# Queue order in a hybrid DeltaNet/attention block: weight splits paced by the piece in use, gate Silu behind attention, decayed keys before the inverse, normed outputs turned later

## The chip, the cores and the metric

The kernel runs on one core of one Trainium2 chip. The metric is the device time of one execution in microseconds (us); lower is better. The core has TensorE (PE, matmuls, with its weight loads shown apart as PEld), VectorE (DVE), ScalarE (ACT), GpSimd (POOL) and SyncE (SP, which here only issues DMAs). Each engine works through its own queue in order. Which engine does a thing is written in the kernel; in which order the instructions lie in a queue is settled when the program is built, by a scheduler that takes earlier parts of the program first where several are ready.

## The reference, cut to what matters

One residual block over 512 tokens of width 1024, in float32:

```python
x = x + 0.5 * g1 * swiglu(modulate(x, sh1, s1), ffn1_w_in, ffn1_w_out)
h = modulate(x, sh2, s2)                       # RMSNorm * (1 + scale) + shift
proj = h @ w_in                                # splits: gq gk gv gz ga gb cq ckv kr
# group A, gated DeltaNet, 4 heads of 128
q, k, v = silu(causal_conv(gq, gk, gv));  q, k = l2norm(q), l2norm(k)
o_a = gated_delta_rule(q, k, v, g, beta)       # chunk form: inverse, u = T v, w = T k, recurrence over chunks
o_a = rms(o_a, gdn_norm_w) * silu(gz)
# group B, latent attention, 4 heads, block-causal
o_b = rms(softmax(q_b k_b^T) v_b, mla_out_norm_w)
x = x + g2 * (concat(o_a, o_b) @ w_out)
x = x + 0.5 * g3 * swiglu(modulate(x, sh3, s3), ffn2_w_in, ffn2_w_out)
```

The FFN width is 2816. (shift, scale, gate) come from a linear map of silu(c).

## The kernel before, in words

Activations lie transposed: a tile holds 128 features by 512 tokens. The dense products keep float32 accuracy by splitting each operand into a rounded high part (`fp32r`) and the rest: `mm3` (L302) makes three matmuls for each pair of tiles, high by high, high by low and low by high. A weight piece ("unit", 1024 rows by 128 columns) is loaded by SP into `wr`, and `split_w` (L201) makes it two pieces: a cast on ACT (`wh`, L202) and a subtraction on DVE (`wl`, L203). Each of the three tags has four buffers. `next_unit` (L298) splits the next unit ahead in program order just before it returns the current one; where the split really lies in the queues of ACT and DVE is the scheduler's choice. A dense piece is 24 matmuls (L304 to L306).

The stages in order: FFN1; then the mixer; then FFN2. Within the mixer (L1666) the projection units run in the order latents, keys, queries, values, z gate. While they run, `dense_units` (L971) steps three side lists of generators: `chain` (latent lifts, delta keys and decay, the blockwise inverse, the solves), `deltas` (query products and norms) and `att` (attention). Steps are traced between pieces of dense work, so that PE has something of each.

After the four z units a loop (L1756) runs `chain`, `deltas` and `rest` (attention) until the first two solves are traced, adds steps of `fill` (the output projection of the attention heads, `out_attended`, L1803; one step is three matmuls of 512 columns), and traces the Silu of the four z tiles when attention has been traced in full (`gate_silu`, L1749). Table activations (Exp, Silu) are chained in program order by `table` (L175), so that few table loads are needed.

Then comes the recurrence over four blocks of 128 tokens (L1776 to L1799). Its matmuls keep the order in which they are traced (`matmuls_in_order`, L153). For block p, `recur` (L1402) has two halves: first `w S` and `q S` (L1415, L1423), then the state update and the output (L1430, L1438). After each half come fill steps and steps of `gated`, a list of `gated_out` generators (L1446), one for each block: the first step takes squares and an inverse root (ACT, DVE, and `ry` by pow on POOL, L188); the second scales the output (`on`, DVE, L969); the third turns it on PE (four transposes, L1461), multiplies by gain and gate (`mf`, L1467) and splits it into `mh` and `ml` (L1469, L1470). The generator yields once more after that, so its end takes a fourth step. `gated` and every list of this kind steps its open generators in turn; one that is at its end is dropped by the step that finds it so.

`solve` (L1370) makes for block p the weighted values `vb`, then (for p > 0) the decayed keys `kbg` and (for p < 3) `kd`, all three DVE products recorded at the helper's line L969, then the products with the inverse (L1389, L1398), copied by ACT to `uu` (L1391) and `w` (L1400).

The output projection of the DeltaNet heads follows in two halves of 256 tokens: `out_half` (L1829) inside the recurrence's fill and final flush, `out_rest` (L1843) behind it. A tile of `out_half` is 12 matmuls of 256 columns; two tiles share one wide unit.

`follow` (L137) adds an edge of class NoSync from one instruction to another: it constrains the order in which the queues are laid out, and no semaphore is made for it.

## Time and profile before

| | |
|---|---|
| median of 3 runs | 1080.29 us (1079.97 to 1081.68) |
| the profiled execution | 1081.6 us; span from first to last instruction 1079.9 us |
| mean granted TensorE clock | 0.997 |
| idle time of PE in the span | 22 us of 1079.9 |
| mixer's stages, us from the span's start | latents and lifts 403 to 487; queries, values, z gate with attention and inverse to about 620; end of attention and solves to 649; recurrence to 684; output halves to about 710; then FFN2 |

A row of a group reads: line, engine, operation, what is written and read, count, then busy time and mean duration of one, then the idle time of the engine just before and who ended it. A row of the waits reads: who waited, for whom, us in total, how often, the longest. A row of the timeline reads: start, duration, engine, line, operation, tiles, count, and in brackets the engine's idle time before it and what ended that. Matmuls are pipelined, so a matmul's duration is longer than the distance to the next one's start.

### The profile page before, as it was taken

What the parts mean: (1) busy time and instruction counts of PE and PEld (TensorE: products, weight loads), DVE (VectorE), ACT (ScalarE), POOL (GpSimd) and SP (SyncE); (2) the same over time, 40 slices, a digit from 0 to 9 for tenths busy, and PEclk for the clock granted to TensorE, in tenths of its full rate; (3) what the DMA queues carried; (4) which work ended last, traced back from release to release, by engine and by line L of the source; (5) the groups of instructions that cost most, each with busy time, mean ns of one, the idle gap of its engine ahead of it and who ended that gap; (6) DMA issues with size and microseconds to landing.
All of it is one profiled execution on the core that took longest, in us unless ns stands there. A gap on an engine that the chain in (4) does not pass through costs nothing.

```text
span 1079.9 us, 14096 instructions
## 1 busy us (share of the span) xinstructions
PE 1057.4 (98%) x5601; PEld 881.9 (82%) x5601; DVE 566.7 (52%) x1000; ACT 383.9 (36%) x641; POOL 25.8 (2%) x74
## 2 busy tenths in 40 slices
PE   6999999999999999999999989999999999999998
PEld 4788878788887798888788778998888888888887
DVE  4478983433586437559797477573333333322220
ACT  3342222222222226465855553352222222222220
POOL 1000000000000000100000002000000000000000
PEclk8999999999999999999999999999999999999999
DMA  9979973233697335210332121004333333333320
GB/s 273 276 219 317 291 217 107 80 96 93 202 289 260 93 88 162 79 39 20 79 88 55 38 75 41 26 22 135 98 98 97 96 95 95 90 100 108 100 71 30
DMA packets 207760, 130.59 MB, mean 121 GB/s; under 512 B 13633, under 2 KB 191822, under 8 KB 207694
## 3 DMA queue, kind: packets, MB, share of 16 engines
q1 hardware_dynamic: 207694, 129.69, 41.2%
q8 instruction: 44, 0.72, 0.3%
q14 instruction: 22, 0.18, 0.1%
HBM read 127.18 MB, written 2.49 MB: 120 GB/s over the span
## 4 chain that ended last, share of the span: by engine, by line
PE 91%; DVE 5%; ACT 1%; DMA 1%; POOL 1%; issue 1%; SPq 0%; ACTq 0%; POOLq 0%
PE pa L304 26%; PE pa L306 26%; PE pa L305 26%; PE pb L1635 1%; PE pb L1615 1%; DMA ar<-in_w_ada 1%; PE pb L305 1%; PE pb L304 1%; PE pb L306 1%; PE pb L453 1%; PE pb L527 1%; PE pb L1237 1%; POOL ry L188 1%; DVE cv L1181 1%; DVE wl L203 0%
## 5 line engine op out<-in xcount | busy, mean ns | idle before, releaser
L202 ACT CAST wh<-wr 128x1024 fp32r<-128x1024 f32 (+1 forms) x164 | 166.9, 1020 | 482.9 <-PE pa L305 322.7
L304 PE MATMUL pa<-hh,wh 128*128 128x512 f32 (+1 forms) x837 | 324.9, 388 | 0.4 <-DVE cv L1181 0.4
L306 PE MATMUL pa<-hh,wl 128*128 128x512 f32 (+1 forms) x837 | 322.0, 385 | 1.4 <-DVE wl L203 1.4
L305 PE MATMUL pa<-hl,wh 128*128 128x512 f32 (+1 forms) x837 | 321.8, 384 | 1.1 <-DVE hl L490 1.1
L203 DVE TENSOR_TENSOR wl<-wr,wh 128x1024 fp32r<-128x1024 f32 (+1 forms) x164 | 194.3, 1187 | 231.1 <-ACT wh L202 225.4
L304 PEld LDWEIGHTS pa<-hh,wh 128*128 128x128 f32 x837 | 157.4, 188 | 34.3 <-issue 2.9
L306 PEld LDWEIGHTS pa<-hh,wl 128*128 128x128 f32 x837 | 157.4, 188 | 32.5 <-DVE wl L203 2.1
L305 PEld LDWEIGHTS pa<-hl,wh 128*128 128x128 f32 x837 | 157.5, 188 | 30.5 <-DVE hl L490 1.4
L304 PE MATMUL pa<-ah,wh 128*128 128x512 f32 (+1 forms) x396 | 146.3, 370 | 0.0
L306 PE MATMUL pa<-ah,wl 128*128 128x512 f32 (+1 forms) x396 | 144.9, 366 | 0.0
L305 PE MATMUL pa<-al,wh 128*128 128x512 f32 (+1 forms) x396 | 144.8, 366 | 0.0
L304 PEld LDWEIGHTS pa<-ah,wh 128*128 128x128 f32 x396 | 74.7, 189 | 13.5 <-ACT wh L202 1.7
L306 PEld LDWEIGHTS pa<-ah,wl 128*128 128x128 f32 x396 | 74.7, 189 | 12.2
L305 PEld LDWEIGHTS pa<-al,wh 128*128 128x128 f32 x396 | 74.7, 189 | 11.9
L658 DVE TENSOR_TENSOR af<-sg,pa 128x512 f32<-128x512 f32 x40 | 27.5, 686 | 103.0 <-PE pa L306 103.0
L612 DVE SCALAR_TENSOR_TENSOR aa<-ar,sc,aa 128x512 f32<-128x512 f32 x98 | 73.2, 750 | 14.5 <-DMA ar<-in_w_ada 13.4
L720 DVE SCALAR_TENSOR_TENSOR xT<-pa,mod,xT 128x512 f32<-128x512 f32 (+1 forms) x18 | 12.4, 692 | 50.1 <-PE pa L306 49.9
L660 ACT CAST ah<-af 128x512 fp32r<-128x512 f32 x44 | 27.4, 622 | 19.7 <-DVE af L658 19.7
L304 PE MATMUL pa<-mh,wh 128*128 128x256 f32 (+1 forms) x96 | 32.6, 341 | 0.0
L305 PE MATMUL pa<-ml,wh 128*128 128x256 f32 (+1 forms) x96 | 30.9, 322 | 0.3 <-DVE ml L1663 0.3
L661 DVE TENSOR_TENSOR al<-af,ah 128x512 fp32r<-128x512 f32 x44 | 30.2, 686 | 1.5 <-ACT ah L660 1.4
L306 PE MATMUL pa<-mh,wl 128*128 128x256 f32 (+1 forms) x96 | 30.7, 320 | 0.0
(375 smaller groups left out, 1076.9 us busy)
## 6 DMA issues: line engine op xcount, KB each, us to landing
wr<-in_ffn_w_in SPq DMA_DIRECT2D x79, 512.0 KB, 3.9
ar<-in_w_ada SPq DMA_DIRECT2D x48, 512.0 KB, 6.2
wr<-in_ffn_w_out SPq DMA_DIRECT2D x32, 512.0 KB, 4.1
ar<-in_w_ada SPq DMA_DIRECT2D x48, 256.0 KB, 5.1
wr<-in_w_in SPq DMA_DIRECT2D x21, 512.0 KB, 3.8
wr<-in_ffn_w_out SPq DMA_DIRECT2D x16, 384.0 KB, 4.5
wr<-in_w_out SPq DMA_DIRECT2D x8, 512.0 KB
wr<-in_ffn_w_in SPq DMA_DIRECT2D x8, 384.0 KB, 7.3
```

What stands on the lines that cost most here:

```text
L188: nc.gpsimd.tensor_tensor(out=y, in0=v, in1=self.mhalf[:, :n], op=ALU.pow)
L202: self.nc.scalar.copy(hi, raw)
L203: self.nc.vector.tensor_tensor(out=lo, in0=raw, in1=hi.bitcast(F32), op=ALU.subtract)
L304: mm(out, wh, xh, start=start, stop=False)
L305: mm(out, wh, xl, start=False, stop=False)
L306: mm(out, wl, xh, start=False, stop=stop)
L453: nc.tensor.matmul(pg[32 * q:32 * q + 32, :256], self.sc[:, kc:kc + 1].to_broadcast([P, 32]), a[:, kc], start=(e == 0), stop=(e == 1), til ...
L612: nc.vector.scalar_tensor_tensor(out=acc, in0=a, scalar=sc, in1=acc, op0=ALU.mult, op1=ALU.add)
L658: nc.vector.tensor_tensor(out=a, in0=s, in1=pu, op=ALU.mult)
L660: nc.scalar.copy(ah, a)
L661: nc.vector.tensor_tensor(out=al, in0=a, in1=ah.bitcast(F32), op=ALU.subtract)
L720: nc.vector.scalar_tensor_tensor(out=self.xT[t][:, ts], in0=p[:, ts], scalar=gate[:, t:t + 1], in1=self.xT[t][:, ts], op0=ALU.mult, op1=AL ...
```

## The change

Four things, all in the order of queues; no arithmetic is added or dropped.

1. From the latents' first three pieces on (`paced`), the cast and the subtraction of each weight split follow the last dense matmul traced so far (`dense_mm`).
2. The Silu of the z tiles follows the last activation of the attention heads' output (`att_end`).
3. The decayed keys `kbg` and `kd` leave `solve` for a generator of their own, `decayed_keys`, added to `deltas` before the loop of L1756; `solve` waits in tracing until they have been traced.
4. In the recurrence `gated` is stepped once per half of `recur` instead of twice, ahead of the fill steps instead of behind them; after the last block it is stepped once more, and then five fill steps instead of four come ahead of the flush.

```diff
-    def table(self, *args, **kw):
+    def table(self, *args, after=None, **kw):
         ins = self.nc.scalar.activation(*args, **kw).ins
+        if after:
+            self.follow(ins, after)
...
     def split_w(self, raw, hi, lo):
-        self.nc.scalar.copy(hi, raw)
-        self.nc.vector.tensor_tensor(out=lo, in0=raw, in1=hi.bitcast(F32), op=ALU.subtract)
+        a = self.nc.scalar.copy(hi, raw)
+        b = self.nc.vector.tensor_tensor(out=lo, in0=raw, in1=hi.bitcast(F32), op=ALU.subtract)
+        if self.paced:
+            self.follow(a.ins, self.dense_mm)
+            self.follow(b.ins, self.dense_mm)
...
-        mm(out, wl, xh, start=False, stop=stop)
+        self.dense_mm = mm(out, wl, xh, start=False, stop=stop).ins.name
...
             ps = self.first_units([self.next_unit(ahead=0) for _ in range(3)], (0, 0, 2), norms)
+        self.paced = True
...
+    def decayed_keys(self):
+        h4 = lambda x: x.rearrange("p (h d) -> p h d", h=4)
+        for p in range(NB):
+            c4 = slice(4 * p, 4 * p + 4)
+            if p > 0:
+                self.kbg[p] = self.slot(s="kbg")
+                self.mul(h4(self.kbg[p]), h4(self.kt[p]), self.bc(self.eG[:, c4], 4))
+            if p < NB - 1:
+                self.kd[p] = self.slot(s="kd")
+                self.mul(h4(self.kd[p]), h4(self.kt[p]), self.bc(self.kcd[:, c4], 4))
+            self.turned = p + 1
+            yield
...
-        kt = self.kt[p]
-        if p > 0:
-            kbg = self.slot(s="kbg")
-            self.mul(h4(kbg), h4(kt), self.bc(self.eG[:, c4], 4))
-        if p < NB - 1:
-            self.kd[p] = self.slot(s="kd")
-            self.mul(h4(self.kd[p]), h4(kt), self.bc(self.kcd[:, c4], 4))
+        while self.turned <= p:
+            yield
+        kbg = self.kbg[p]
         yield
...
-        nc.scalar.activation(mh, pt, AF.Copy, scale=gain)
+        self.att_end = nc.scalar.activation(mh, pt, AF.Copy, scale=gain).ins.name
...
+        deltas.add(self.decayed_keys())
         gates = list(self.zT)
 
         def gate_silu(n):
-            silu(gates[:n])
+            silu(gates[:n], self.att_end)
...
                 for _ in self.recur(p):
                     loosely(chain, 2)
                     loosely(rest, 4)
+                    gated.step()
                     if not rest.open and not rest.todo:
                         fill.step(3)
-                    gated.step(2)
                 gated.add(self.gated_out(p))
                 gated.step()
...
             while rest.open or rest.todo:
                 loosely(rest, 1)
-            fill.step(4)
+            gated.step()
+            fill.step(5)
             gated.flush()
             fill.flush()
```

More of the change, by code (lines that the diff above doesn't have):

```diff
@@ L102, in __init__ @@
         self.tabled = None
+        self.paced = False
     def name(self, s):
@@ L1684, in conv_done, with silu @@
             return f
-        def silu(tiles):
+        def silu(tiles, after=None):
             for t in tiles:
-                self.table(t, t, AF.Silu)
+                self.table(t, t, AF.Silu, after=after)
         self.inv = [None] * NB
-        self.kd, self.us, self.o, self.wk = ([None] * NB for _ in range(4))
+        self.kd, self.kbg, self.us, self.o, self.wk = ([None] * NB for _ in range(5))
+        self.turned = 0
         self.S = None
```

## The prediction, made before the change was run

> **What bounds the kernel now.** I read the page first: busy shares and groups.

> ```profile
> span 1079.9 us, 14096 instructions
> PE 1057.4 (98%) x5601; PEld 881.9 (82%) x5601; DVE 566.7 (52%) x1000; ACT 383.9 (36%) x641; POOL 25.8 (2%) x74
> L202 ACT CAST wh<-wr 128x1024 fp32r<-128x1024 f32 (+1 forms) x164 | 166.9, 1020 | 482.9 <-PE pa L305 322.7
> L203 DVE TENSOR_TENSOR wl<-wr,wh 128x1024 fp32r<-128x1024 f32 (+1 forms) x164 | 194.3, 1187 | 231.1 <-ACT wh L202 225.4
> ```

> TensorE (PE) is busy 98% of the span, and the change takes no matmul away. All that can be won is the 22 us in which PE is idle, and all that can be lost is new idle time. So the second view is the waits of PE alone, of which these rows belong to the mixer:

> ```profile
> PE pb L1461 <- DVE on L969: 1.9, 3, 1.0
> PE pb L1635 <- ACT pT L1631: 1.7, 1, 1.7
> PE pa L306 <- DVE wl L203: 1.4, 1, 1.4
> PE pb L1657 <- DVE on L969: 0.8, 1, 0.8
> PE pb L1389 <- DVE vb L969: 0.8, 2, 0.4
> PE pa L304 <- DVE cv L1181: 0.4, 1, 0.4
> PE pa L305 <- DVE ml L1663: 0.3, 1, 0.3
> ```

> Together 7.3 us: the ceiling of any gain, 0.7% of the time. The third view is the windows by stage (columns: PE, PEld, DVE, ACT, POOL busy, clock, DMA share and rate):

> ```profile
> 441.00:487.00 46.00, 46.00 (x229) 39.60 (x229) 23.16 (x52) 27.25 (x52) 2.00 (x2) 1.00 0.17 46
> 487.00:517.00 30.00, 29.36 (x146) 23.19 (x144) 29.37 (x85) 16.79 (x32) 1.02 (x1) 1.00 0.07 18
> 597.00:649.00 52.00, 48.37 (x409) 37.96 (x409) 30.79 (x65) 28.94 (x61) 2.01 (x2) 1.00 0.22 62
> 740.00:1040.00 300.00, 300.00 (x1335) 248.41 (x1334) 96.91 (x102) 80.50 (x102) 0.00 (x0) 1.00 0.34 99
> ```

> PE idles in 487 to 517 (where DVE is busy 29.37 of 30 us: DVE bounds that stretch) and 3.6 us in 597 to 649. From 740 to 1040, FFN2, it has no idle time at all. The L1461 waits lie in the recurrence after that.

> **Gate Silu behind the attention.** On ACT, and PE's row after it:

> ```profile
> 621.31 1.28 ACT L177 ACT_TABLE_LOAD   x1
> 622.61 2.19 ACT L177 ACTIVATE z<-z 128x512 f32<-128x512 f32 x4
> 625.23 0.35 ACT L1631 COPY pT<-pb 128x256 f32<-128x256 f32 x1
> 625.63 0.71 PE L1635 MATMUL pb<-vn,pT 128*128 128x128 f32 x4 [1.67 <-ACT pT L1631]
> 635.83 0.69 ACT L1662 ACTIVATE mh<-pb,cwT 128x512 fp32r<-128x512 f32 x1 [4.36 <-PE pb L1657]
> 640.21 0.58 ACT L1391 COPY uu<-pb 128x512 f32<-128x512 f32 x1 [0.54 <-PE pb L1389]
> ```

> The table load and four Silus hold ACT for 3.5 us (621.31 to 624.80) with attention's copies queued behind them; PE waits 1.7 for one. Tied behind the last L1662 they start some 1.7 earlier than 636.5 and are over by 638.3, about when the first uu copy, then also 1.7 earlier (638.5), wants ACT. Queued behind them are only splits that nobody waits for yet, and z is first read by the turned outputs of the recurrence. Cover gone, it would cost up to the block, 3.5; I take none. Gain 1.7. Two later waits of attention, 0.8 and 0.3, have a chain that begins at those copies; PE arrives earlier too, so I take 0.3 of 1.1.

> **Decayed keys ahead of the inverse.** Three kd and three kbg products:

> ```profile
> L969 DVE TENSOR_TENSOR kbg<-ktk,eG x3: 674/676/676, 640.5 to 645.9; 128x512 f32<-128x512 f32 x3
> L969 DVE TENSOR_TENSOR kd<-ktk,kcd x3: 673/677/677, 639.3 to 643.5; 128x512 f32<-128x512 f32 x3
> ```

> They are 4.1 us of DVE between the vb products that PE awaits. `deltas` steps once a turn, so they go to the first turns, and DVE has 21 idle us in 597 to 649 to take them. They hold two slots more than before (each replaces its ktk, but blocks 1 and 2 need both). The vb waits go: gain 0.8. If the slots delay attention it could be nothing.

> **Normed outputs turned later.**

> ```profile
> 661.65 1.22 DVE L203 TENSOR_TENSOR wl<-wr,wh 128x1024 fp32r<-128x1024 f32 x1
> 661.82 1.92 POOL L188 TENSOR_TENSOR ry<-ve,mhalf 128x4 f32<-128x4 f32 x1 [1.11 <-DVE ve L1452]
> 673.88 0.66 PE L1461 MATMUL pb<-ident,on 128*128 128x128 f32 x4 [0.97 <-DVE on L969]
> 678.71 1.01 POOL L188 TENSOR_TENSOR ry<-ve,mhalf 128x4 f32<-128x4 f32 x1 [5.61 <-DVE ve L1452]
> 680.59 0.63 PE L1461 MATMUL pb<-ident,on 128*128 128x128 f32 x4 [0.30 <-DVE on L969]
> 678.69 0.28 PE L304 MATMUL pa<-mh,wh 128*128 128x256 f32 x1
> 678.81 0.28 PE L305 MATMUL pa<-ml,wh 128*128 128x256 f32 x1
> ```

> Following the generators: `gated_out` has three yields and its end takes a fourth step. With single steps, block 0 is scaled in `recur(1)`'s first half and turned after its second; block 0's end eats a step, so block 1 is turned in `recur(3)`'s first half, blocks 2 and 3 only in the final flush. Each L1461 group then has at least a half of `recur` and three fill steps more between it and its product: over 2 us against waits of 0.97 at most. Block 3 gets one tile of out_half more: 12 matmuls at 0.12 (678.69 to 678.81), 1.4, against 0.30. Gain 1.9.

> Here one pow takes 1.92 beside a weight subtraction and 1.01 alone. [...]

> The price lies behind it: out_half's splits. Unit 97's split may now only follow tile 1 and is needed at tile 4, while blocks 2 and 3 bring DVE this:

> ```profile
> L1467 DVE SCALAR_TENSOR_TENSOR mf<-pb,cwT,z x16: 341/344/352, 656.2 to 682.7; 128x128 f32<-128x128 f32 x16
> L1470 DVE TENSOR_TENSOR ml<-mf,mh x16: 281/284/293, 657.0 to 683.5; 128x128 fp32r<-128x128 f32 x16
> 688.18 0.48 DVE L1825 SCALAR_TENSOR_TENSOR xT<-pa,mod,xT 128x256 f32<-128x256 f32 x1 [1.40 <-PE pa L306]
> ```

> Eight mf and eight ml, 5.0 us, all earlier in the program than wl 97. From tile 1's end PE has two groups of turns (0.9) and two tiles at 1.88 (the update's 0.48 and the 1.40 before it), 4.7 in all. DVE needs 5.0, two xT updates (0.96) and 1.2 for wl: 7.2, less overlap of back-to-back instructions (16 times some 0.08, 1.3) and what ACT's gaps let through. Late by 0 to 2; I take 0.7.

> **Weight splits tied behind the piece in use.** The edge orders queues when they are laid out; the chip gets no new semaphore. Before, a split ran as soon as one of four wh buffers came free, three units ahead of its use; now unit n+1's comes after unit n-1's last matmul, one unit ahead. In FFN2 that is free: 300 us over 1335 matmuls is 0.225 each, 24 of them 5.4 us of cover for 1.02 + 1.19 on ACT and DVE, both under a third busy. The last columns, at 0.12 each, still give 2.9. SP's loads move with the splits that free their wr buffers and keep four units of lead. The stage that matters is 487 to 517 (the first row is the window before it, of the wl instructions alone: PE, PEld, DVE):

> ```profile
> 441.00:487.00 46.00, 12.21 (x31) 5.82 (x31) 5.38 (x5) 1.00 0.17 46
> 502.42 0.48 PE L306 MATMUL pa<-hh,wl 128*128 128x512 f32 x1
> 502.83 0.75 DVE L1181 SCALAR_TENSOR_TENSOR cv<-pa,cwT,cv 128x511 f32<-128x511 f32 x1
> 506.35 0.74 DVE L1181 SCALAR_TENSOR_TENSOR cv<-pa,cwT,cv 128x509 f32<-128x509 f32 x1
> 508.03 1.06 ACT L202 CAST wh<-wr 128x1024 fp32r<-128x1024 f32 x1 [5.00 <-PE pa L305]
> 517.05 1.21 DVE L203 TENSOR_TENSOR wl<-wr,wh 128x1024 fp32r<-128x1024 f32 x1
> 518.31 0.50 PE L306 MATMUL pa<-hh,wl 128*128 128x512 f32 x1 [1.43 <-DVE wl L203]
> ```

> Before, five subtractions ran in 441 to 487, where DVE is half idle, those of the four query units among them, and the next was that of 517.05. Now two of them, 2.4 us, fall into the stretch that DVE already fills. The one for the third query unit comes right behind the first unit's convolution (502.83 to 507.1) in program order, and PE wants it at 502.42. As a filler like the convolution's first step, which DVE took at 502.83, it starts 1.2 later at 504.0 and ends at 505.2: 2.8 idle. In that idle time DVE catches up, and the waits of 1.4 and 0.4 at the end of the stretch go. Net cost 1.0. Best end: it fits between, and those 1.8 go: a gain of 1.8. Worst end: it runs behind the convolution's last step at 507.1, plus 1.2 for the other one and 1.2 itself: 509.5, 7.1 idle, nothing given back. In the tie's favour: ACT no longer sits 5.00 us at a split whose buffer PE holds. But PE waited for no copy queued behind it, only for DVE.

> **The sum.** -1.7 - 0.3 - 0.8 - 1.9 + 0.7 + 1.0 = -3.0 us. The profiled execution took 1081.6 (1079.9 and 1.7 around it), 1.3 over the median; 1078.6 after it, 1077.3 against the median of 1080.3.

> **The rivals.**
> *Pacing costs nothing*: ACT's unblocked queue feeds DVE sooner and the subtractions find gaps. For it: ACT's 5.00. Against: DVE busy 29.37 of 30. -4.7 + 0.7 - 1.8 = -5.8: 1074.5.
> *The stalls refill*: chains, not queues, set the ends of attention and solve, so half of the 4.7 comes back as waits on the next link. For it: waits of 0.3 to 0.8 sit right behind the 1.67 already. Against: DVE and ACT both idle there. -2.35 + 0.7 + 1.0 = -0.7: 1079.6.
> *Slower: the paced subtraction starves PE among the query units*, at the worst end above. -4.7 + 0.7 + 7.1 = +3.1: 1083.4; it makes the kernel slower from 6.2 us of such idle time on. For it: DVE full, and the wl of 517.05 was already late for PE. Against: DVE's order there already mixes urgent and idle work.
> That the tie does nothing is the first term at 0, inside the forecast's range.

> **How the numbers follow.** Forecast 0.40 (own range 1075.5 to 1079.5), costless 0.22, refill 0.20, slower 0.18. A measurement tells 0.2%, 2.2 us: faster is below 1078.1, slower above 1082.5. Three quarters of the forecast's 0.40 lie below 1078.1: faster 0.52, same 0.30, slower 0.18. Range 1073.0 to 1084.5: it leaves out half of the slower case and the tail of the costless one.

> **What would show it.** Silu: table load after the last L1662, and no wait of L1635 on pT. Keys: kd and kbg before 630, no wait of L1389 on vb. Turns: L1461 waits for nothing, two groups of it side by side in the final flush. Pacing: subtractions spread over 487 to 517, PE's wait on wl earlier than 510 and some 3 us long; a short one at out_half's fifth tile. I am wrong if PE idles over 6 us in 487 to 529, if FFN2 shows any wait on wl, or if L1461 still waits.

## The result, and the profile after

The changed kernel takes 1087.91 us (median of 4 runs, 1086.75 to 1088.89) against 1080.67 for the kernel before on the same chip: 1.0062 times as long, interval 1.0049 to 1.0075. The forecast was 1077.3 and its range ended at 1084.5. So the kernel became 7 us slower where 3 us less were expected. The profiled execution took 1088.89 us, its span is 1087.2, its mean granted clock 0.989 (before: 1079.9 and 0.997).

The waits of TensorE in the mixer, after the change. The added lines shift the numbers: L311 to L313 are the dense matmuls, L1189 the convolution's steps, L1479 the turn of the normed outputs, L1407 the solve's first products, L1681 the low part of an attention head, L976 the helper of products.

```profile
PE pa L311 <- DVE cv L1189: 3.0, 1, 3.0
PE pb L1479 <- DVE on L976: 2.5, 1, 2.5
PE pb L1407 <- DVE vb L976: 1.6, 1, 1.6
PE pa L312 <- DVE ml L1681: 1.2, 1, 1.2
```

Of the seven rows before, the three turns (1.9), pT (1.7), wl (1.4) and cv (0.4) are gone as they were, 5.4 us. In their place stand the rows above. With the small ones (0.4, 0.3 and 0.2 on other products) the mixer's waits come to 9.2 us against 7.3: only 1.9 of the 7.3 us by which the span grew.

The rest is in a column that the prediction read as a constant. The windows by stage (us; busy time and instructions of PE, PEld, DVE, ACT and POOL; granted clock; DMA share and rate), and for the three places where the clock changes:

```profile
487.00:517.00 30.00, 26.61 (x122) 21.10 (x121) 29.33 (x83) 15.64 (x29) 1.02 (x1) 0.89 0.19 53
510.30:517.10 6.80, 5.55 (x17) 4.60 (x18) 6.68 (x14) 1.68 (x4) 0.00 (x0) 0.50 0.27 77
636.60:643.40 6.80, 6.59 (x28) 4.99 (x27) 1.77 (x3) 4.05 (x6) 0.72 (x1) 0.50 0.00 0
687.80:691.20 3.40, 2.78 (x13) 2.81 (x14) 3.40 (x10) 1.22 (x6) 0.00 (x0) 0.50 0.06 17
740.00:1040.00 300.00, 300.00 (x1332) 248.45 (x1332) 95.06 (x105) 80.70 (x102) 0.00 (x0) 1.00 0.34 99
```

In three stretches, five times 3.41 us or 17.1 together, TensorE's granted clock is 0.50; before, these stages stood at 1.00 throughout. (The 0.997 of before comes from 6.8 us at 0.50 in its first 23 us, which the changed kernel has too.) Each stretch begins within one of the waits above or just behind it: cv (508.5 to 511.5), ml (635.0 to 636.2), on (685.9 to 688.4). PE can look busy in such a stretch (6.59 of 6.80), because its work takes longer at half clock: the turn in the last row of this section takes 1.09 us, such a group before 0.63 to 0.66. At half clock 17.1 us lose at most 8.5 us of matmul time; what is left after the waits, 7.3 - 1.9 = 5.4, fits under that. All of the loss lies in the mixer: the same PE work comes 0.6 us earlier than before at 460 us and 7.4 later where FFN2 begins. FFN2 (740 to 1040) is what it was: no idle time with one unit of lead.

How the waits arise, in rows of the timeline. The two paced subtractions on DVE and what PE then awaits; the last block's scaling on DVE and the turn that awaits it:

```profile
492.18 1.22 DVE L207 TENSOR_TENSOR wl<-wr,wh 128x1024 fp32r<-128x1024 f32 x1
495.74 1.22 DVE L207 TENSOR_TENSOR wl<-wr,wh 128x1024 fp32r<-128x1024 f32 x1
...
510.66 0.74 DVE L1189 SCALAR_TENSOR_TENSOR cv<-pa,cwT,cv 128x509 f32<-128x509 f32 x1
511.55 0.77 PE L311 MATMUL pa<-hh,wh 128*128 128x512 f32 x1 [3.04 <-DVE cv L1189]
...
685.94 0.87 DVE L1485 SCALAR_TENSOR_TENSOR mf<-pb,cwT,z 128x128 f32<-128x128 f32 x3
...
687.39 0.28 DVE L1488 TENSOR_TENSOR ml<-mf,mh 128x128 fp32r<-128x128 f32 x1
687.59 0.69 DVE L976 TENSOR_TENSOR on<-o,ry 128x512 f32<-128x512 f32 x1
688.42 1.09 PE L1479 MATMUL pb<-ident,on 128*128 128x128 f32 x4 [2.52 <-DVE on L976]
```

The subtractions moved into 487 to 517, as forecast. They are 2.4 us of DVE work ahead of the convolution's steps, and these steps free the accumulator (`pa`) that the next piece needs. In the flush, block 3's scaling (687.59) lies behind the gating of block 2 (from 685.94), which itself waited for PE to turn block 2.

### The profile page after: what moved, and what is told of

Its sections match the earlier page's. It is cut to its first block, busy times and chain, and to the rows that moved or that the text cites. A ratio compares the mean times of both kernels' runs of the same rounds, so it can differ in the third digit from the quotient of the medians.

```text
span 1087.2 us, 14098 instructions
## 1 busy us (share of the span) xinstructions
PE 1064.5 (98%) x5601; PEld 888.8 (82%) x5601; DVE 563.1 (52%) x1000; ACT 383.0 (35%) x641; POOL 26.4 (2%) x74
## 4 chain that ended last, share of the span: by engine, by line
PE 91%; DVE 5%; DMA 1%; ACT 1%; issue 1%; SPq 0%; POOL 0%; DVEq 0%; ACTq 0%
PE pa L311 26%; PE pa L312 26%; PE pa L313 26%; PE pb L311 1%; PE pb L312 1%; PE pb L313 1%; DVE cv L1189 1%; PE pb L460 1%; PE pb L1653 1%; PE pb L1633 1%; PE pb L534 1%; DVE wl L207 1%; PE pb L1245 0%; DMA xt<-in_x 0%; PE pb L1407 0%
## 5 line engine op out<-in xcount | busy, mean ns | idle before, releaser
L311 PE MATMUL pa<-hh,wh 128*128 128x512 f32 (+1 forms) x837 | 326.1, 390 | 3.1 <-DVE cv L1189 3.0
L313 PE MATMUL pa<-hh,wl 128*128 128x512 f32 (+1 forms) x837 | 322.4, 385 | 0.0
L311 PEld LDWEIGHTS pa<-hh,wh 128*128 128x128 f32 x837 | 158.0, 189 | 37.0 <-ACT qrT L1566 3.5
L313 PEld LDWEIGHTS pa<-hh,wl 128*128 128x128 f32 x837 | 157.8, 189 | 31.2 <-DVE wl L207 0.4
L311 PE MATMUL pa<-ah,wh 128*128 128x512 f32 (+1 forms) x396 | 146.3, 369 | 0.0
L313 PE MATMUL pa<-ah,wl 128*128 128x512 f32 (+1 forms) x396 | 144.9, 366 | 0.0
L311 PEld LDWEIGHTS pa<-ah,wh 128*128 128x128 f32 x396 | 74.7, 189 | 13.6 <-ACT wh L206 1.7
L313 PEld LDWEIGHTS pa<-ah,wl 128*128 128x128 f32 x396 | 74.7, 189 | 12.2
L663 ACT ACTIVATE sg<-pa 128x512 f32<-128x512 f32 x44 | 26.1, 594 | 63.0 <-PE pa L313 63.0
L1189 DVE SCALAR_TENSOR_TENSOR cv<-pa,cwT,cv 128x511 f32<-128x511 f32 (+2 forms) x36 | 26.8, 746 | 22.2 <-ACT cv L1187 21.8
L311 PE MATMUL pa<-mh,wh 128*128 128x256 f32 (+1 forms) x96 | 33.7, 353 | 0.0
L798 ACT COPY o<-pb 128x512 f32<-128x512 f32 (+1 forms) x9 | 4.9, 540 | 81.3 <-PE pb L796 81.3
```

The lines of the kernel that those rows point to most:

```text
L311: mm(out, wh, xh, start=start, stop=False)
L313: self.dense_mm = mm(out, wl, xh, start=False, stop=stop).ins.name
L663: nc.scalar.activation(s, pg, AF.Silu)
L1189: nc.vector.scalar_tensor_tensor(out=a[:, d:], in0=p[:, :NT - d], scalar=wj(3 - d), in1=a[:, d:], op0=ALU.mult, op1=ALU.add)
```

## The experiments

Theory: each of the four parts shifts work on an in-order engine so that TensorE meets a new wait, and a wait of some 2 us costs more than itself, because the granted clock then falls to half for 3.4 us or more (as behind the waits of 3.0, 1.2 and 2.5 above: 6.8, 6.8 and 3.4 us). Rivals: pacing alone makes the loss (the prediction's own slower case); or the parts are harmless alone and only hurt together. Every ratio is to the kernel before, measured beside it on the same chip; its median lay between 1080.6 and 1082.0 us. A ratio with its interval can differ from the quotient of the two medians by 0.1%.

**Pacing alone.**

```
+            self.follow(a.ins, self.dense_mm)
+            self.follow(b.ins, self.dense_mm)
```

> Only the first of the four edits: the splits paced. Theory 1 (the loss starts in the stretch that DVE fills, and the clock doubles it): two subtractions again lie between 487 and 511, PE again waits about 3 us for the third step of a convolution, the granted clock is 0.5 for some 6.8 us behind that wait, and PE's excess over back-to-back matmuls between 500 and 520 grows from 3.5 to about 7 us; the whole run is 3 to 5 us slower than before (1084 to 1086). Rival (the tie is harmless, the loss comes from what lies later, keys and turns): 1079 to 1081.5, no stretch at 0.5 after 400.

Measured 1084.36 us (1083.53 to 1087.68), ratio 1.0036 (1.0020 to 1.0052). One row of its waits and two of its windows:

```profile
PE pa L308 <- DVE cv L1186: 3.0, 1, 3.0
```

```profile
490.00:511.70 21.70, 18.16 (x90) 14.10 (x89) 21.22 (x68) 10.34 (x17) 1.02 (x1) 1.00 0.18 49
511.70:515.10 3.40, 3.33 (x10) 2.74 (x11) 3.31 (x8) 1.16 (x2) 0.00 (x0) 0.50 0.57 154
```

The wait is 3.0 for 1.8 that vanish, so 1.2 net; all waits of the mixer come to 9.7 for 7.3, so 2.4 net. The 3.40 us at half clock cost up to 1.7 more: together up to 4.1. The medians differ by 3.1, and the ratio makes 3.9. Waits and clock both have a share, and the runs do not divide it more finely. The spans of the two profiled executions differ by only 2.7, because the one of before has half clock at its start and this one has not; counted from 460 us on, this one is 4.5 longer.

**Silu alone.**

```
-            silu(gates[:n])
+            silu(gates[:n], self.att_end)
```

> Only the gate Silu behind the attention. Theory 1: the wait of 1.7 us on the copied probabilities is gone and little comes in its place; 1.0 to 2.0 us faster (1078.5 to 1079.5), clock never 0.5 after 400. Rival (chains set the end of attention, so the wait goes over to the next link): within 0.7 us of before.

Measured 1080.92 us (1079.91 to 1085.18), ratio 0.9997 (0.9983 to 1.0011). The wait on pT is gone and the wait on vb is longer. PE's row, and DVE ahead of it:

```profile
636.70 1.41 DVE L1816 SCALAR_TENSOR_TENSOR xT<-pa,mod,xT 128x512 f32<-128x512 f32 x2 [0.88 <-PE pa L308]
638.03 0.68 DVE L967 TENSOR_TENSOR fl<-fr,fh 128x512 fp32r<-128x512 f32 x1
638.63 0.68 DVE L971 TENSOR_TENSOR vb<-pb,kn 128x512 f32<-128x512 f32 x1
639.46 2.33 PE L1391 MATMUL pb<-vb,U 128*128 128x128 f32 x16 [1.65 <-DVE vb L971]
```

PE arrives earlier, but vb lies in DVE's queue behind two updates of xT that wait for PE's own matmuls. The waits on vb grow from 0.8 to 2.0. The stall refills: the prediction's second rival, for this part.

**Decayed keys alone.**

```
+        deltas.add(self.decayed_keys())
```

> Only the decayed keys in a generator of their own. Theory 1: the six products no longer lie at 639 to 646 but at 625 to 634, ahead of DVE's work for the end of attention, so the waits of 0.8 us on vb turn into waits of 1 to 2.5 us on ml and on, with the clock at 0.5 for 3.4 us or more if they come close together; 0 to 3 us slower (1080.5 to 1083.5). Rival (the forecast's own step: DVE has room there): 0.8 us faster, 1079.5.

Measured 1083.23 us (1080.95 to 1084.92), ratio 1.0026 (1.0014 to 1.0039). DVE before the row of PE that waits, and the two windows around the end of the wait:

```profile
629.84 0.68 DVE L969 TENSOR_TENSOR kbg<-ktk,eG 128x512 f32<-128x512 f32 x1
...
631.36 0.73 DVE L1673 SCALAR_TENSOR_TENSOR ml<-pb,cwT,mh 128x512 fp32r<-128x512 f32 x1
632.15 0.50 PE L305 MATMUL pa<-ml,wh 128*128 128x512 f32 x1 [1.88 <-DVE ml L1673]
```

```profile
630.84:634.25 3.41, 1.32 (x5) 0.83 (x6) 2.35 (x6) 0.00 (x0) 1.01 (x1) 1.00 0.00 0
634.25:637.67 3.42, 3.42 (x19) 2.79 (x19) 1.48 (x3) 1.20 (x2) 0.00 (x0) 0.50 0.00 0
```

The products are made between 619 and 630, five of them from 624 on, near the end of attention, and `ml` queues behind them. The wait on ml grows from 0.3 to 1.9, the waits on vb (0.8) go, and 3.4 us at half clock cost up to 1.7: up to 2.5 in all, 2.8 by the ratio.

**Late turn alone, and the same with one line moved.**

```
-                    gated.step(2)          (behind fill.step(3))
+                    gated.step()           (ahead of it)
...
+            gated.step()
+            next(gated.open[-1])           (only in the repaired one: block 3's scaling)
+            fill.step(5)
```

> Only the normed outputs turned later, with the weight splits as before. Theory 1: the waits of the four-transpose groups on the scaled outputs (1.9 us) are gone, and the last block's scaling is not held up, because no weight subtraction falls into the flush: 1.5 to 2 us faster (1078.3 to 1079), clock never 0.5 after 400. Rival (the late turn itself puts the last block's scaling behind the block before it on DVE): a wait of 2 to 2.5 us between two transpose groups, clock 0.5 for 3.4 us, within 1.5 us of before.

> The late turn alone, with one line moved: the last block's scaling is traced right behind the recurrence, ahead of block 2's turn and of the five fill steps. If the 2.5 us wait came from the order on VectorE (block 2's gating, an xT update and a weight subtraction ahead of the scaling), the wait falls under 0.5 and the kernel gains what the prediction had for the turns, 1.5 to 2 us: about 1079.5 against 1081.2 before. If the scaling is late by its own chain (squares, pow), or block 2's gating and the output halves only move back behind it, the wait stays over 1.5 or a new one of that size appears, and the time stays within 0.5 us of before.

Late turn: 1081.02 us (1079.04 to 1086.26), ratio 1.0003 (0.9988 to 1.0018). Three waits of together 1.9 us become one of 2.5, with the same order on DVE as in the changed kernel; in this profile the turn behind it takes 0.63, where it took 1.09 at half clock. Repaired: 1078.12 us (1076.12 to 1082.97), ratio 0.9975 (0.9960 to 0.9989), and no wait on `on` in the recurrence is left. The late turn's row of PE, then DVE in the repaired kernel:

```profile
681.36 0.63 PE L1461 MATMUL pb<-ident,on 128*128 128x128 f32 x4 [2.52 <-DVE on L969]
```

```profile
675.45 0.69 DVE L969 TENSOR_TENSOR on<-o,ry 128x512 f32<-128x512 f32 x1 [1.18 <-POOL ry L188]
...
676.72 1.22 DVE L203 TENSOR_TENSOR wl<-wr,wh 128x1024 fp32r<-128x1024 f32 x1
...
678.64 0.86 DVE L1467 SCALAR_TENSOR_TENSOR mf<-pb,cwT,z 128x128 f32<-128x128 f32 x3
```

Now `on` (675.45) stands ahead of the weight subtraction and of block 2's gating. The order of a single instruction of 0.69 us was the difference between nothing and 2.7 us, of which 1.9 are the waits that went; the rest lies inside the interval (1.2 to 4.3).

**Where pacing costs: switched on later, or with two units of lead.**

```
-        self.paced = True                  (behind the latents' first pieces)
+        self.paced = True                  (behind the Silu of the queries)
```

```
+            if self.gone:                  (the dense matmul that stood at the split before)
+                self.follow(a.ins, self.gone)
+                self.follow(b.ins, self.gone)
+            self.gone = self.dense_mm
```

> Pacing alone, but switched on only after the query units (behind their Silu) and not after the latents' first pieces. If the loss of pacing is that two weight subtractions fall among the VectorE work beside the query units, it is gone: within 1 us of the kernel before, no wait of TensorE on the convolution near 511 us over 0.6, and no half clock behind it. If one unit of lead is too short anywhere in the mixer (values, z gate, output halves), a good part of the +3 stays, and shows as waits on wl behind 517 us.

> Pacing alone, but each split follows the last dense matmul that stood when the split before it was traced: two units of lead in place of one. If the loss is the lead (one unit of 5.4 us is shorter than the block of work on VectorE among the queries and on ScalarE among the values), it goes: within 1 us of before, no wait of TensorE on cv, wh or wl that before did not have, no half clock. If any tie that moves splits out of the latents' stretch costs it, some 3 us over before stay.

Later: 1086.74 us (1084.74 to 1088.11), ratio 1.0049 (1.0030 to 1.0068), no better than pacing from the start (the intervals overlap), so the first branch fell. PE's waits and ACT's row ahead of them:

```profile
534.15 4.89 ACT L1271 COPY bd<-at 32x128 f32<-32x128 f32 x16
539.65 1.03 ACT L203 CAST wh<-wr 128x1024 fp32r<-128x1024 f32 x1
540.73 0.50 PE L308 MATMUL pa<-hh,wh 128*128 128x512 f32 x1 [1.83 <-ACT wh L203]
542.50 0.71 PE L310 MATMUL pa<-hh,wl 128*128 128x512 f32 x1 [1.04 <-DVE wl L204]
```

Here the cast is held, behind 16 small copies on ACT that take 4.89 us together, and half clock follows from 542.63 to 546.04. Two units of lead: 1082.79 us (1081.06 to 1085.82), ratio 1.0020 (1.0011 to 1.0029), with full clock behind the two waits shown here (eight products of L1245 take 1.06 at 520.42):

```profile
PE pb L1172 <- ACT nT L1500: 1.4, 1, 1.4
PE pa L311 <- DVE cv L1189: 1.2, 1, 1.2
```

By the ratios the second unit of lead takes away nearly half of pacing's loss, though the intervals overlap. Two subtractions still run in the full stretch of DVE (at 491.64 and 494.92), and waits of 1.2 and 1.4 stand there for the 1.8 of before. That the rest of the loss stays as long as a subtraction is moved there at all fits this, but was not tried by itself. Neither branch of the expectation holds alone.

**Where the keys have room.** Three more places: behind the solve's first products, ahead of the queries' products, and ahead of the loop that ends attention.

```
         nc.scalar.copy(self.us[p], pu)
+        kt = self.kt[p]                    (kbg and kd made here)
```

```
-        deltas.add(self.delta_qk(kT, qT), self.delta_q(qT))
+        deltas.add(self.decayed_keys(), self.delta_qk(kT, qT), self.delta_q(qT))
```

```
-        deltas.add(self.decayed_keys())
+        drain(self.decayed_keys())
```

> Neither before's place of the decayed keys nor the change's: the keys are traced inside the solve, behind its first four products with the inverse. If the 0.8 us of waits on vb are there because the keys of block 1 lie ahead of the next block's vb on VectorE, they go, with no wait on ml at the end of attention: 0.5 to 0.8 us less than before and no half clock. If instead the w products then wait for kbg, it comes back there as 0.5 or more, and the time is that of before.

> The decayed keys alone, in their own generator as in the change, but handed to the list ahead of the queries' products, so that they are made among the value units. If the idea is right and only its place at the end of attention cost the 2 us, the waits on vb go (0.8) and no wait on ml over 0.4 comes: 0.5 to 1 us less than before, no half clock near 635. If the keys only find another full stretch of VectorE, a wait of TensorE of 0.5 or more appears between 520 and 600 and the time is that of before or worse.

> The decayed keys alone, all six products traced ahead of the loop that ends attention and the inverse, so that VectorE can take them in its idle time between 597 and 619 us. If VectorE has a free place there, the waits on vb (0.8) go, no wait on ml over 0.4 and none of the inverse's products over 0.5 comes: 0.5 to 1 us less than before. If the inverse's small VectorE steps between 600 and 615 are the path, six products of 0.68 ahead of them delay the solve, waits of 0.5 or more on U or vb appear, and the time is that of before or up to 2 us more.

Behind the products: 1084.42 us (1082.68 to 1086.14), ratio 1.0024 (1.0010 to 1.0038); the w products wait 1.9 for the last kbg, which stands behind 2.48 us of another step on DVE. Ahead of the queries' products: 1084.50 (1083.10 to 1086.24), ratio 1.0033 (1.0022 to 1.0044). Ahead of the loop: 1079.66 (1078.09 to 1083.70), ratio 0.9991 (0.9979 to 1.0002). One row of each of the first two, and the groups of the third:

```profile
PE pb L1398 <- DVE kbg L969: 2.2, 2, 1.9
```

```profile
573.78 0.69 DVE L969 TENSOR_TENSOR t<-t,mk 128x512 f32<-128x512 f32 x1 [4.41 <-DMA t<-t_d]
588.51 1.13 PE L1318 MATMUL pb<-t,at 128*128 128x128 f32 x8 [2.42 <-DVE ve L1659]
```

```profile
L969 DVE TENSOR_TENSOR kd<-ktk,kcd x3: 682/683/685, 619.6 to 622.0; 128x512 f32<-128x512 f32 x3
L969 DVE TENSOR_TENSOR kbg<-ktk,eG x3: 683/683/684, 620.2 to 622.6; 128x512 f32<-128x512 f32 x3
```

Among the value units the 4.1 us of keys (at 545 to 552) stand ahead of the chain that feeds the inverse: its first step ran at 569.69 in the kernel before and runs at 573.78 here, 4.1 later, and PE waits 2.42 for a later one. (This profile also has half clock behind the wait on wl that the kernel before has too: eight products of L1237 take 1.79 at 520.51, and 1.06 at 526.09.) Ahead of the loop the six products run side by side in 619.6 to 623.3, where VectorE has nothing urgent, and the waits on vb go with nothing in their place: the 0.8 that the prediction had. The ratio makes it 1.0, with an interval that just includes no change.

**Parts together.**

```
A pacing, B Silu, C keys, D turn, d turn repaired, l keys ahead of the loop
no_pace: B C D    all_fix: A B C d    no_pace_fix: B C d
fix_silu: B d     fix_silu_keys: B d l     fix_keys: d l
```

> The whole change without its pacing: Silu, keys and turns. If the parts add, the excess of the keys alone (+2.0 us) is what is left: about +1.8 us over before, with one half clock stretch of 3.4 us near 635. If the parts worsen each other (waits on ml and on vb within one stretch, wait on the scaled output behind them), it stays +4 us or more over before with half clock near 637 and near 688, as in the changed kernel, and pacing is worth only the +3 that it costs alone.

> The whole change with the last block's scaling traced ahead of block 2's turn. The turn's own repair was worth 2.7 us alone. If the parts add, the changed kernel loses 2.5 to 3 by it: about 1085. If the wait on the scaled output was also what halved the clock near 688 in the changed kernel, it loses 4 to 5: about 1083.5. Slower than before by 2.5 to 4 either way, by the pacing and the keys.

> The whole change without its pacing and with the repaired turn. The same without the repair was 0.7 us over before; the repair was worth 2.7 alone and 4 in the whole change. If the parts add: 1.5 to 2.5 less than before, 1078.3 to 1079.3, with the waits on ml (1.2) and vb (1.6) still there. If these two waits halve the clock in most executions, it comes no lower than 1080.

> The repaired turn with Silu behind the attention. If the parts add, Silu's zero leaves the 2.7 us of the repaired turn: 1078.0. If Silu's wait on vb was worse only because the late turn or the fill steps behind it were in the way, up to 1 us more: 1077.

> The repaired turn, Silu behind the attention, and the keys ahead of the loop. If the wait on vb that Silu left (1.65) is made by the keys of the block before lying ahead on VectorE, it falls to under 0.6 and the kernel gains 1 us over the same without the keys: 1077. If it is made by the xT updates of the fill steps, it stays, and the time is that of the repaired turn with Silu or worse.

> The repaired turn (2.7 us alone) and the keys ahead of the loop (0.9 to 1.2 alone), nothing else of the change. If they add: 3.5 to 4 us less than before, about 1077. If they share a wait, no better than the repaired turn alone, 1078.

| kernel | median us (range) | ratio (interval) | waits of PE that matter |
|---|---|---|---|
| B C D | 1081.52 (1078.78 to 1086.06) | 1.0008 (0.9991 to 1.0026) | on 2.5, vb 1.6, ml 1.2 |
| A B C d | 1083.65 (1081.11 to 1084.85) | 1.0025 (1.0016 to 1.0034) | cv 3.0, vb 1.7, ml 1.2 |
| B C d | 1078.70 (1075.73 to 1084.47) | 0.9988 (0.9972 to 1.0004) | vb 1.4, ml 1.2 |
| B d | 1078.02 (1076.96 to 1082.89) | 0.9977 (0.9965 to 0.9990) | vb 2.0 |
| B d l | 1078.34 (1076.64 to 1081.32) | 0.9982 (0.9971 to 0.9992) | vb 1.7, T 1.1 |
| d l | 1076.66 (1074.93 to 1081.99) | 0.9959 (0.9945 to 0.9973) | T 1.7, where it was pT before |

By the ratios, taking pacing out of the changed kernel is worth almost 6 us (1.0062 to 1.0008) where it costs 3.9 alone, and repairing the changed kernel's turn is worth 4 (1.0062 to 1.0025) where it is worth 3 in the late turn; neither difference is beyond the intervals. In the trace of A B C d the half clock near 688 is gone with the wait on `on`: the clock is 0.94 in 487 to 517 and 0.93 in 597 to 649, so some 3.4 and 6.8 us at half, and its mean of 0.995 over 1081.8 us leaves no room for another. B C D has three of the waits of the changed kernel to a tenth, yet its profile has a mean clock of 1.000 and a span of 1077.0; the spans of other executions reach 1084.3 at a clock of 0.994. In time it is the first branch of its expectation, in waits the second. B C d gains 1.3 with an interval that includes no change, less than expected; its executions are spread from 1.000 to 0.991 in clock. B d adds as expected. In B d l the wait on vb stays with the keys out of its way, which leaves the updates of xT that stood ahead of vb in Silu's own run. d and l add up to 4.4 us less than before: the lowest ratio of the study, without pacing and without Silu, though its interval overlaps that of d alone.

**The opposite of pacing: one unit more of lead**, on top of d and l.

```
-            u, p = self.next_unit(), self.acc()
+            u, p = self.next_unit(ahead=2), self.acc()
```

> The same, and in the units of keys, queries, values and z each split traced one unit earlier, two units ahead of its use. If program order decides which work VectorE takes first in the full stretch, the split that TensorE awaited at 518 (1.43 us, with 0.4 of cv before it) comes sooner: 1 to 1.8 us less than the same without it, and fewer executions with a half clock there. If an earlier split only pushes the convolution steps back, a wait on cv grows by what the wait on wl loses, or more: no gain, or up to 2 us slower.

1078.87 us (1076.56 to 1081.30), ratio 0.9976 (0.9963 to 0.9988), against 0.9959 without it: no gain, and the intervals overlap. The waits on wl and cv near 516 go, but the inverse's first products wait instead, as with the early keys:

```profile
PE pb L1318 <- DVE t L969: 1.7, 1, 1.7
```

**A ladder of idle stretches**, to see when the clock falls.

```
+            self.idle(pu, 2 * ((f - 2) % 10))   (FFN2: a chain of DVE copies, then a transpose that waits for it)
```

> The kernel before with twenty idle stretches made for TensorE in FFN2, one behind each pair of units from the third pair on: a VectorE copy of the last product, then 0, 2, 4 ... 18 more copies of 128x128 one behind the other, and a transpose that waits for them, with all later products behind it; the ladder runs twice. It shows by itself when the granted clock falls to half. If what counts is the share of a stretch of about 3.4 us in which TensorE idled, and where the wait lies against it, the shortest waits never halve the clock, those over some 3 us always do, and between 1.2 and 2.8 us the two ladders differ at the same length. If a fixed length of one wait decides (between the 2.5 that did nothing and the 3.0 that did), both ladders change at the same step, and the halving behind 1.9 in the keys' run needs another cause.

One execution, 1202.89 us, with twenty waits from 0.4 to 7.1 us, so the ladder was steeper than meant. Four rows of PE, then stretches of 3.41 us between which the clock changes:

```profile
771.14 0.33 PE L806 MATMUL pb<-ident,hole 128*128 128x128 f32 x1 [2.44 <-DVE hole L805]
804.23 0.33 PE L806 MATMUL pb<-ident,hole 128*128 128x128 f32 x1 [3.96 <-DVE hole L805]
939.78 0.30 PE L806 MATMUL pb<-ident,hole 128*128 128x128 f32 x1 [2.53 <-DVE hole L805]
971.41 0.44 PE L806 MATMUL pb<-ident,hole 128*128 128x128 f32 x1 [4.05 <-DVE hole L805]
```

```profile
767.98:771.39 3.41, 0.97 (x6) 0.51 (x5) 2.54 (x7) 1.54 (x2) 0.00 (x0) 1.00 0.17 51
771.39:774.80 3.41, 3.41 (x10) 2.64 (x10) 0.99 (x2) 0.62 (x1) 0.00 (x0) 0.50 0.52 154
774.80:778.21 3.41, 3.41 (x17) 2.80 (x16) 0.00 (x0) 0.00 (x0) 0.00 (x0) 1.00 0.00 0
935.23:938.64 3.41, 2.02 (x9) 1.32 (x8) 1.25 (x5) 1.54 (x2) 0.00 (x0) 1.00 0.51 149
938.64:942.05 3.41, 2.27 (x11) 1.93 (x12) 2.28 (x4) 0.62 (x2) 0.00 (x0) 1.00 0.37 108
942.05:945.47 3.42, 3.42 (x17) 2.84 (x16) 0.00 (x0) 0.07 (x1) 0.00 (x0) 1.00 0.18 50
798.70:802.11 3.41, 1.57 (x7) 0.95 (x6) 1.70 (x5) 1.54 (x2) 0.00 (x0) 1.00 0.41 123
802.11:805.52 3.41, 1.29 (x6) 1.11 (x7) 2.56 (x8) 0.62 (x1) 0.00 (x0) 1.00 0.49 135
805.52:808.93 3.41, 3.41 (x9) 2.63 (x8) 0.00 (x0) 0.00 (x0) 0.00 (x0) 0.50 0.08 23
965.95:969.36 3.41, 1.41 (x7) 0.83 (x5) 1.86 (x5) 1.54 (x2) 0.00 (x0) 1.00 0.41 121
969.36:972.77 3.41, 1.36 (x4) 1.20 (x5) 2.40 (x8) 0.62 (x1) 0.00 (x0) 0.50 0.51 150
972.77:976.19 3.42, 3.42 (x9) 2.65 (x9) 0.00 (x0) 0.00 (x0) 0.00 (x0) 0.50 0.01 3
```

The changes of the clock in these rows lie multiples of 3.413 us apart (771.39, 805.52 ten of them later, 969.36 another 48 later). 2.44 us of idle time within one such stretch were followed by 0.50; 2.53 us, the same rung of the second ladder, fall over two (1.39 and 1.14), and 1.00 followed both; of 3.96 the first part (1.84) was followed by 1.00, the second (2.12) by 0.50; of 4.05 both (2.00 and 2.05) were followed by 0.50. So in these rows, among dense matmuls, the most idle time of 3.41 that had full clock behind it is 1.84, and the least that had half clock 2.00. The half stretch from 771.39 begins 8 matmuls and the full one behind it 15, so a half stretch costs some 7 times 0.226, 1.6 us. So the first branch holds: the same wait is free or costs some 1.6 us more, by where it falls.

## Why the prediction was wrong

**All that can be lost.** The prediction's first step, "all that can be lost is new idle time", failed. New idle time is 1.9 of the 7.3 us that the profiled span grew by. The rest fits the 17.1 us at half clock, up to 8.5. The clock was in no term and no rival, though its column stood in the windows quoted: 0.001 of the mean clock of a span of 1080 us is 2.2 us at half rate, which is up to 1.1 us. The changed kernel's 0.989 against 0.997 makes up to 8.6 by that rule. The ceiling of "7.3 us" bounded the gain, and nothing was set up that bounded the loss. The waits, too, came out the other way: 3.0 us less were forecast, 1.9 more were found, by the terms below. One of the prediction's own signs of being wrong came: L1461, now L1479, still waits.

**Silu, -1.7 and -0.3.** The stall went where it was said to go (table load at 640.03, behind the last `mh`; no wait on pT). The step that failed is "Gain 1.7", which took the end of that wait as time won and left the next wait, on vb, as it was. In the run alone vb grew from 0.8 to 2.0, since it queues on DVE behind work that waits for PE, and the two later waits of attention stayed at 0.8 and 0.3. Worth 0, not 2.0.

**Keys, -0.8.** The failed step is "`deltas` steps once a turn, so they go to the first turns, and DVE has 21 idle us in 597 to 649". They did go one block a turn, but these turns lie at 619 to 630 (625 to 635 in the changed kernel), and even traced ahead of the loop the products began only at 619.6. What DVE had idle before that was out of reach from there, and idle time summed over 52 us is no place. With the place made by hand the waits on vb went, 0.8; by the change's own place, alone, the loss was 2.8.

**Turns, -1.9.** The failed step is "Each L1461 group then has at least a half of `recur` and three fill steps more": the prediction saw that blocks 2 and 3 both turn in the flush and costed block 2's gating against a weight split, +0.7, but not against block 3's own scaling, which stands behind the same gating. Alone 0; with that one instruction traced earlier -2.7. The +0.7 did not show.

**Pacing, +1.0.** That the idle time of this stretch came to 1.2 net is luck, since the wait was another one. The failed step is that the subtraction "starts 1.2 later at 504.0" and PE waits for it: the subtractions ran early, at 492.18 and 495.74, and PE waited 3.0 for the convolution's steps (cv) that came behind them. FFN2 waited for nothing, as said. The term also lacked what goes with the wait, 3.4 us at half clock alone and 6.8 in the changed kernel. The slower rival had the place and asked for 6.2 us of idle time; 3.0 with the clock behind it cost 3.9 alone. The costless rival fell with its premise: the subtractions found no gap.

Left open: which small waits halve the clock in the mixer. Idle time within a stretch of 3.41 us does not settle it there. In the changed kernel a wait of 1.25 lies whole in the one ahead of the change (633.19 to 636.60, PE busy 2.16), and half clock follows; in B C D the wait on ml is 1.2 as well, and none follows (mean clock 1.000). The stretch ahead of the half clock had PE busy 1.32 us of 3.41 in the keys' run, 1.63 in B C d:

```profile
631.51:634.92 3.41, 1.63 (x6) 0.68 (x5) 2.62 (x7) 0.00 (x0) 1.01 (x1) 1.00 0.00 0
634.92:641.75 6.83, 6.58 (x27) 5.49 (x28) 1.93 (x4) 5.06 (x8) 0.00 (x0) 0.50 0.00 0
```

The 1.63 is more than the 1.57 behind which the ladder kept full clock, and the 2.16 more than its 2.02. These stretches hold other matmuls beside the wait than the ladder's, in the changed kernel mostly small ones (64x64); what that does was not tried by itself. By their ratios the parts alone (3.9, -0.3, 2.8 and 0.3) add up to 6.7, and together they make 6.7 as well, so the rival that they only hurt together falls.

## What to carry to other kernels

Before moving work on an in-order engine, list what stands behind it in that queue at the new place, instruction by instruction: a sum of idle time is no place, and one scaling of 0.69 us traced in the wrong order undid a gain of 2.7. A lead of one piece is enough where the engines are a third busy (in FFN2 DVE 95 and ACT 81 of 300 us, and TensorE without a wait) and too short beside a block nearly as long as the piece (4.89 us of copies against 5.4). On a TensorE that is 98% busy, price a wait near 2 us with the clock it may take away: here 3.4 or 6.8 us at 0.50, so up to another 1.7 us or twice that.

## What the runs showed of the hardware

The same program differs from one execution to the next; no run here shows why. B C d ran at spans from 1074.0 us at a mean clock of 1.000 to 1082.8 at 0.991; the kernel before at 1076.9 to 1078.7 where its clock was 1.000 and up to 1084.2 at 0.991. Part of this lies in the first 25 us, which no part of the change touches: the profiles of the kernel before and of the changed one have 6.8 us of half clock there, those of B C D and of d and l with one unit more of lead none (mean clock 1.000). So single times of such kernels are compared only beside their clocks, and small differences from a stage on, not from the start.
